# Constants of an S5 branch on GpSimd alone and half-swapped key and query rows in a one-core decoder step

## The chip, the cores and the metric

One core of a Trainium2 chip runs the whole program. The metric is device time in microseconds (us), the median of several runs; one further execution was profiled. All products are float32 in and out.

## The reference, cut to what matters

A hybrid decoder layer is computed for one prompt (16 meta tokens and 512 tokens) and, with the same weights, for 8 single-token samples: a normalised x times a wide input weight gives queries, keys, values, an S5 input u and gates; the two branches are merged through gates and two output weights, and a last weight leads back to x.

```python
h = jnp.einsum('btd,de->bte', rmsnorm(x, norm_gain), w_in)      # 2048 -> q, k, v, z_a, u, z_s, g_a, g_s
q = rope(rmsnorm(q, q_norm_gain), pos); k = rope(rmsnorm(k, k_norm_gain), pos)
...
x1 * cos - x2 * sin, x2 * cos + x1 * sin                        # rope: the two halves of a head cross
...
lam_bar = jnp.exp(lam * dt)                                     # the constants of the S5 branch
b_bar = ((lam_bar - 1.0) / lam)[..., None] * lax.complex(b_re, b_im)
a_cum, h = lax.associative_scan(ssm_combine, (a, bu), axis=1)
...
br_a = (o_attn * jax.nn.silu(z_a)) @ w_attn_out
br_s = (y_ssm * jax.nn.silu(z_s)) @ w_ssm_out
return x + (jax.nn.sigmoid(g_a) * br_a + jax.nn.sigmoid(g_s) * br_s) @ w_out
```

Attention is over a window of 128 positions, the 16 meta tokens and a sink.

## The kernel before, in words

Every float32 product is three matmuls of rounded parts: ScalarE casts a weight to a high part (whi), VectorE subtracts it to get the low part (wlo), and TensorE multiplies high by high, high by low and low by high. The weights come as 176 units of 512 KB through SP's queue into three buffers (`Stream`, L961 to L963) and each is used for 48 matmuls of 260 columns.

The stages on TensorE, one after the other: blocks of plain products (`mm`, L1116); from 114 to 394 us thirteen "quads" (`Quads`, `quad`, L1319), in which seven products do the work of eight: sums of weight tiles are made on VectorE (L1024) and sums of x, the "taus", ahead of time (`taus`, L1378 to L1398); then again plain blocks (q, k, v heads, u, gates), beside which the S5 scan and, from 754 us on, the attention run; the output weights; a last group of quads.

Work beside the products is written as generators in the lanes of a `Background` (L906). Every 24 matmuls `bg.step(budget)` runs the lanes on until the costs they yield use up a budget (`BUDGET2` to `BUDGET4` from the attention on); `yield None` ends a lane's turn in that step. So where a piece of background work stands in the order of each engine is set by the costs and budgets, and each engine and each queue goes through its list in order. The loads and splits of weights have a higher priority (`HIGH`) and go in front.

What the change and the prediction touch: `ssm_prep` (L143) makes the constants of the S5 branch during the quads, tensor_tensor and tensor_scalar on GpSimd and everything else (scalar_tensor_tensor, reciprocal) on VectorE, through the class `Mostly` (L30); in its middle TensorE transposes F (L225), and the result goes out through SP (L231). `again` (L1428) then stores the constants that are kept (983 KB) on SP's queue (L1430). `heads` (L1270) writes each block of q, k or v rows to DRAM (`rawD`, L1277); `Attn.load` (L619) reads a block back (`sb`), once more with the 32-row quarters exchanged in pairs (`sw`, four pieces, L628), and the norms (`rb`, L631); `rope` (L637) combines the three, `queries` (L709) makes QT (L718, L719), and `scores` (L723) multiplies (L735, L736). `sample_heads` (L556) does the same for the samples on GpSimd's queue. `attention` (L1516) orders all this.

```python
# in attention()
         at.load_q(0)
         yield None
         for kv in range(4):
             yield from at.queries(kv)
             yield from at.blocks(kv, kv == 3)
```

Of the kernel before, what the change touches and what calls it, by code (L numbers as in the profile page):

```python
# [8 lines left out]
F32 = mybir.dt.float32  # L9
# [3 lines left out]
ALU = mybir.AluOpType  # L13
# [13 lines left out]
    return a.to_broadcast(s)  # L27


class Mostly:  # L30


    def __init__(self, a, b):
        self.a, self.b = a, b

    def __getattr__(self, name):
        return getattr(self.a if name in ("tensor_tensor", "tensor_scalar", "tensor_copy", "memset") else self.b, name)


def acc_exp(v, pool, out, x, n):  # L40
# [73 lines left out]

def spots():

    r, o = {("early", "size"): 704, ("prod", "size"): 512, ("late", "size"): 256, ("pow", "size"): 192}, 0
    for nm, n in (("ex_c", 32), ("ex_k", 32), ("ex_r", 32), ("ex_q", 32), ("ex_i", 32), ("sc_n", 64), ("sc_k", 64), ("sc_r", 64),
                  ("sc_s", 64), ("sc_q", 64), ("f_g", 64), ("f_m", 32), ("f_t", 32), ("f_n", 32)):
        r[nm] = ("early", o)  # L120
        o += n
    r["nta"] = ("early", 0)
    for nm, o in (("c96_1", 0), ("c96_2", 192), ("ct1", 0), ("ct2", 256)):
        r[nm] = ("prod", o)
    for nm, o in (("fts", 0), ("Z", 0), ("zc", 64), ("zc2", 128), ("n32a", 192)):
# [16 lines left out]

def ssm_prep(nc, K, tmp, psum, dram, R, ident, a_prm, later):  # L143

    v = Mostly(nc.gpsimd, nc.vector)
    prm = K["prm"]
    nc.sync.dma_start(out=prm, in_=a_prm)
    are, aim, ldt = prm[:, 0], prm[:, 1], prm[:, 2]
    dt = tmp.tile([P, 32], F32, name="dt")
    acc_exp(v, tmp, dt, ldt, 32)  # L150
    yield 3.0
# [43 lines left out]
    m2 = tmp.tile([P, 32], F32, name="f_m")
    t = tmp.tile([P, 32], F32, name="f_t")
    v.tensor_tensor(out=m2, in0=are, in1=are, op=ALU.mult)
    v.tensor_tensor(out=t, in0=aim, in1=aim, op=ALU.mult)
    v.tensor_tensor(out=m2, in0=m2, in1=t, op=ALU.add)
    v.reciprocal(out=m2, in_=m2)  # L200
# [15 lines left out]
    nF = K["nF"]  # L216
    v.tensor_scalar(out=nF, in0=fv[:, :, 0], scalar1=-1.0, scalar2=None, op0=ALU.mult)
    yield 2.5
    for _ in range(6):
        yield None  # L220
    ft = psum.tile([P, 512], F32, name="tr")
    fts = tmp.tile([P, 2, P], F32, name="fts")
    with later():
        for h in range(2):
            nc.tensor.transpose(out=ft[:, 128 * h:128 * h + 128], in_=Fk[:, 4 * h:4 * h + 4].rearrange("p k a -> p (k a)"),  # L225
                                identity=ident)
    yield 0.0
    yield None
    nc.scalar.copy(out=fts.rearrange("p h s -> p (h s)"), in_=ft[:, 0:256])
    FD = dram.tile([8, 32, P], F32, name="FD")  # L230
    nc.sync.dma_start(out=FD.rearrange("(h k) a s -> (k a) h s", h=2), in_=fts)  # L231
    R["FD"] = FD
    yield 0.0
# [322 lines left out]
def sample_heads(nc, pool, dram, smc, idn, raw, rk, rq, ps, later):  # L556

    v = nc.vector
    x, sw, rb = (pool.tile([P, 12, 8], F32, name=n, bufs=1) for n in ("x12", "s12", "r12"))
    qs, kvs = (pool.tile([P, n, 8], F32, name=nm, bufs=1) for nm, n in (("qs", 8), ("kvs", 4)))  # L560
    for c in range(2):
        cols = slice(4 * c, 4 * c + 4)
        src = raw[:, :, c, 264:268].rearrange("n p j -> p n j")
        nc.gpsimd.dma_start(out=x[:, :, cols], in_=src)
        for q in range(4):
            b = 32 * (q ^ 1)
            nc.gpsimd.dma_start(out=sw[32 * q:32 * q + 32, :, cols], in_=src[b:b + 32])
# [36 lines left out]
class Attn:  # L604
# [14 lines left out]
    def load(self, i, W, row):  # L619

        nc, pool = self.nc, self.pool
        cs = slice(CH - W, CH)
        sb = pool.tile([P, 2, W], F32, name="sb")
        nc.sync.dma_start(out=sb, in_=self.raw[i][:, :, cs])
        sw = pool.tile([P, 2, W], F32, name="sw")
        for q in range(4):
            b = 32 * (q ^ 1)
            nc.sync.dma_start(out=sw[32 * q:32 * q + 32], in_=self.raw[i][b:b + 32, :, cs])  # L628
        rb = pool.tile([P, 2 * W], F32, name="rb")
        for e in range(2):  # L630
            nc.sync.dma_start(out=rb[64 * e:64 * e + 64], in_=row(e).unsqueeze(0).to_broadcast([64, 2 * W]))  # L631
        return sb, sw, rb
# [52 lines left out]
    def values(self, e):  # L685
        nc, pool = self.nc, self.pool
        sb = pool.tile([P, 2, CH], F32, name="sv")
        nc.sync.dma_start(out=sb, in_=self.raw[2 + e])
# [351 lines left out]
def trunk(tc, A, O):  # L1040
# [229 lines left out]
    def heads(i):  # L1270
# [156 lines left out]

    def again():  # L1428

        nc.sync.dma_start(out=kD, in_=flats[0][:, 0:NKEPT])  # L1430
        quarters()
        raw = [qs.more.tile([P, 8, P], F32, name="raw", bufs=3).rearrange("p k n -> p (k n)") for _ in range(3)]
        raw = [raw[n // 3][:, CH * (n % 3):CH * (n % 3) + CH] for n in range(8)]
        for n, r in enumerate(raw):
            nc.sync.dma_start(out=r, in_=A["x"][:, 2 * n, 1])
        yield 0.0
        yield None
        for n, r in enumerate(raw):
            list(xkeep(2 * n, r, 1))
            yield 0.5  # L1440
# [75 lines left out]
    def attention():  # L1516
# [341 lines left out]
```

## Time and profile before

| | us |
|---|---|
| median of 3 runs | 1291.26 (1290.59 to 1296.47) |
| profiled execution, own time | 1291.91 |
| its span | 1290.1 |
| TensorE busy | 1263.1 (98%), 10405 matmuls |
| VectorE busy | 966.4 (75%) |
| ScalarE busy | 622.6 (48%) |
| GpSimd busy | 240.0 (19%) |
| DMA | 215.94 MB, mean 167 GB/s |

The span is the profiled part of one execution; its own time is some 1.8 us longer, and stands 0.65 us over the median. Busy shares are averages over stages that differ, so where time is lost has to be read by stretches. The granted clock of TensorE was 0.991 of full over the span.

### The profile page before, as it was taken

How to read it: one execution, taken by the hardware profiler on the slowest of the kernel's cores; microseconds unless marked ns; L12 is line 12 of the kernel's file. 1: busy time of each engine (PE TensorE's matmuls, PEld its weight loads, DVE VectorE, ACT ScalarE, POOL GpSimd, SP SyncE). 2: the span in 40 equal slices, each digit the busy share in tenths (PEclk: the TensorE clock that was granted, in tenths of full speed). 3: DMA queues.
4: the chain of work that ended last, by engine and by line, in shares of the span. 5: the costliest groups of instructions: out<-in, count | busy, mean ns of one | idle time of the engine just before them, and what ended most of it. 6: DMA issues, size and time to landing. Idle time of an engine off the chain costs nothing.

```text
span 1290.1 us, 26491 instructions
## 1 busy us (share of the span) xinstructions
PE 1263.1 (98%) x10405; PEld 1236.8 (96%) x10405; DVE 966.4 (75%) x1536; ACT 622.6 (48%) x1330; POOL 240.0 (19%) x420
## 2 busy tenths in 40 slices
PE   9999899999999999999999997999999999999998
PEld 9999899999999999999999997999999999999998
DVE  8586598687786578877679648889976567887775
ACT  8554354345455864455522233486556623344442
POOL 0003899700001420122033221111110000000000
PEclk9999899999999999999999998999999999999999
DMA  8544243244346545545454479777874565545441
GB/s 287 201 153 163 91 134 134 103 157 157 114 129 226 175 128 174 160 140 157 132 144 119 136 214 279 225 237 220 234 251 149 166 192 182 181 153 156 143 145 51
DMA packets 104274, 215.94 MB, mean 167 GB/s; under 512 B 21740, under 2 KB 43172, under 8 KB 104116
## 3 DMA queue, kind: packets, MB, share of 16 engines
q1 hardware_dynamic: 95700, 196.83, 47.7%
q0 software_dynamic: 8448, 17.40, 5.6%
q8 instruction: 82, 1.34, 0.5%
q14 instruction: 44, 0.36, 0.1%
HBM read 180.99 MB, written 34.11 MB: 167 GB/s over the span
## 4 chain that ended last, share of the span: by engine, by line
PE 77%; POOL 11%; issue 6%; DMA 3%; ACT 1%; DVE 1%; SPq 1%; POOLq 0%; ACTq 0%; DVEq 0%
PE mm L1116 46%; PE pr L1319 22%; POOL work L69 2%; PE wg L784 2%; POOL work L71 2%; POOL work L70 1%; DMA raw<-in_w 1%; DMA xr<-in_x 1%; PE aux L1116 1%; POOL work L72 1%; POOL work L57 1%; PE aux L1319 1%; POOL work L56 1%; PE wg L515 1%; PE tr L515 1%
## 5 line engine op out<-in xcount | busy, mean ns | idle before, releaser
L1025 ACT CAST whi<-raw 128x1024 fp32r<-128x1024 f32 x147 | 151.9, 1048 | 158.9 <-DVE raw L1024 80.9
L1026 DVE TENSOR_TENSOR wlo<-raw,whi 128x1024 fp32r<-128x1024 f32 x147 | 182.9, 1266 | 56.6 <-ACT whi L1025 56.2
L962 ACT CAST whi<-raw 128x1024 fp32r<-128x1024 f32 (+3 forms) x136 | 130.7, 970 | 171.1 <-PE mm L1116 93.9
L1116 PE MATMUL mm<-xh,whi 128*128 128x260 f32 (+1 forms) x888 | 207.1, 287 | 1.7 <-ACT xr L1174 1.7
L1116 PE MATMUL mm<-xh,wlo 128*128 128x260 f32 (+1 forms) x888 | 205.5, 285 | 0.0
L1116 PE MATMUL mm<-xl,whi 128*128 128x260 f32 (+1 forms) x888 | 204.1, 284 | 0.0
L963 DVE TENSOR_TENSOR wlo<-raw,whi 128x1024 fp32r<-128x1024 f32 (+3 forms) x136 | 152.1, 1126 | 63.1 <-ACT whi L962 53.1
L1319 PE MATMUL pr<-cb,whi 128*128 128x260 f32 x848 | 153.1, 283 | 1.8 <-ACT whi L1025 1.8
L1116 PEld LDWEIGHTS mm<-xh,whi 128*128 128x128 f32 x888 | 147.6, 189 | 5.6 <-issue 2.5
L1319 PE MATMUL pr<-tau,whi 128*128 128x260 f32 x800 | 146.1, 284 | 3.5 <-ACT z L1353 2.3
L1116 PEld LDWEIGHTS mm<-xh,wlo 128*128 128x128 f32 x888 | 147.6, 189 | 1.1 <-issue 1.0
L1116 PEld LDWEIGHTS mm<-xl,whi 128*128 128x128 f32 x888 | 148.0, 189 | 0.0
L1319 PEld LDWEIGHTS pr<-cb,whi 128*128 128x128 f32 x848 | 130.9, 189 | 2.0 <-ACT whi L1025 2.0
L1319 PEld LDWEIGHTS pr<-tau,whi 128*128 128x128 f32 x800 | 123.7, 189 | 3.9 <-ACT z L1353 2.5
L1319 PE MATMUL pr<-cb,wlo 128*128 128x260 f32 x424 | 119.1, 283 | 0.0
L1319 PE MATMUL pr<-tau,wlo 128*128 128x260 f32 x400 | 113.1, 283 | 0.0
L1024 DVE TENSOR_TENSOR raw<-raw 128x1024 f32<-128x1024 f32 x84 | 104.0, 1238 | 8.3 <-DMA raw<-in_w 6.9
L1116 PE MATMUL mm<-Y,whi 128*128 128x260 f32 x576 | 105.9, 288 | 0.3 <-DVE Y L1575 0.3
L1319 PE MATMUL pr<-xh,whi 128*128 128x260 f32 x304 | 85.4, 287 | 3.6 <-ACT whi L1025 3.5
L1116 PEld LDWEIGHTS mm<-Y,whi 128*128 128x128 f32 x576 | 83.8, 188 | 3.4 <-issue 2.7
L1319 PE MATMUL pr<-xh,wlo 128*128 128x260 f32 x304 | 86.3, 285 | 0.6 <-DVE wlo L1026 0.6
L1319 PE MATMUL pr<-xl,whi 128*128 128x260 f32 x304 | 86.1, 285 | 0.0
(421 smaller groups left out, 2968.5 us busy)
## 6 DMA issues: line engine op xcount, KB each, us to landing
raw<-in_w SPq DMA_DIRECT2D x202, 512.0 KB, 4.3
gD<-z SPq DMA_DIRECT2D x38, 260.0 KB, 4.4
t<-gD SPq DMA_DIRECT2D x32, 260.0 KB, 2.8
cache<-in_vc POOLq DMA_DIRECT2D x16, 286.0 KB, 3.9
cache<-in_kc POOLq DMA_DIRECT2D x15, 288.0 KB, 5.9
xr<-in_x SPq DMA_DIRECT2D x16, 268.0 KB, 5.0
xg<-in_x SPq DMA_DIRECT2D x8, 536.0 KB, 4.7
sD<-z SPq DMA_DIRECT2D x16, 260.0 KB, 2.9
```

Of the source, the lines that this page charges most:

```text
L56: v.tensor_tensor(out=q, in0=q, in1=r, op=ALU.mult)
L69: v.tensor_tensor(out=t1, in0=a, in1=bc(br, 1, 2), op=ALU.mult)
L71: v.tensor_tensor(out=out[:, 0], in0=t1[:, 0], in1=t2[:, 1], op=ALU.subtract)
L515: nc.tensor.matmul(o[n], lhsT=D["CL"][:, 2 * e + n, i, 1:5], rhs=H[:, 2 * e + n, i, 0:140], start=False, stop=(i == 1))
L784: nc.tensor.matmul(pv[64 * e:64 * e + 64, 0:256], lhsT=V, rhs=pr[:, e::2], start=(i == 0), stop=(i == len(parts) - 1))
L962: nc.scalar.copy(out=hi, in_=raw)
L963: self.dve = nc.vector.tensor_tensor(out=lo, in0=raw, in1=hi.bitcast(F32), op=ALU.subtract).ins
L1024: nc.vector.tensor_tensor(out=o, in0=o, in1=i, op=ALU.add)
L1025: nc.scalar.copy(out=hi, in_=t)
L1026: nc.vector.tensor_tensor(out=lo, in0=t, in1=hi.bitcast(F32), op=ALU.subtract)
L1116: m = nc.tensor.matmul(ps[:, c, 0:W], lhsT=wt[:, k], rhs=xo(kt, c), start=f, stop=l)
L1319: m = nc.tensor.matmul(bank, lhsT=wt[:, p], rhs=x(p, e), start=first and f and p == 0, stop=l and p == 7, skip_group_check=not first and l ...
```

## The change

- The class `Mostly` becomes `OnPool`: a scalar_tensor_tensor of the constants is now a tensor_scalar and a tensor_tensor, both on GpSimd. The reciprocal of |lambda|^2 stays on VectorE, its input is made first, and seven idle turns stand behind it.
- F's transposes, copy and store go from the middle of the constants to their end, behind eight idle turns.
- The kept constants are stored through GpSimd's queue.
- `rawD` holds each block twice. `heads` stores k and q also with quarters exchanged, in four pieces of 32 partitions; `load` reads both copies with 128 partitions each into one tile `sbw`. `sample_heads` reads the second copy as well.
- The loads of x for the taus stand under an order behind the last background matmul.
- Two idle turns (`NDELAY`) stand between the first queries and the first scores; three budgets are larger.

```diff
-class Mostly:
+class OnPool:
...
+    def scalar_tensor_tensor(self, out, in0, scalar, in1, op0, op1):
+        n = int(np.prod(out.shape[1:]))
+        t = self.tmp.tile([P] + list(out.shape[1:]), F32, name=f"st{n}")
+        self.e.tensor_scalar(out=t, in0=in0, scalar1=scalar, scalar2=None, op0=op0)
+        self.e.tensor_tensor(out=out, in0=t, in1=in1, op=op1)
...
-    v = Mostly(nc.gpsimd, nc.vector)
+    v = OnPool(nc, tmp)
...
+    v.tensor_tensor(out=m2, in0=are, in1=are, op=ALU.mult)
+    v.tensor_tensor(out=t, in0=aim, in1=aim, op=ALU.mult)
+    v.tensor_tensor(out=m2, in0=m2, in1=t, op=ALU.add)
+    yield 0.0
+    for _ in range(7):
+        yield None
+    v_ = nc.vector
+    v_.reciprocal(out=m2, in_=m2)
...
-    for _ in range(6):
-        yield None
-    ft = psum.tile([P, 512], F32, name="tr")
...
+    for _ in range(8):
+        yield None
+    ft = psum.tile([P, 512], F32, name="tr")
...
-        sb = pool.tile([P, 2, W], F32, name="sb")
-        nc.sync.dma_start(out=sb, in_=self.raw[i][:, :, cs])
-        sw = pool.tile([P, 2, W], F32, name="sw")
-        for q in range(4):
-            b = 32 * (q ^ 1)
-            nc.sync.dma_start(out=sw[32 * q:32 * q + 32], in_=self.raw[i][b:b + 32, :, cs])
+        t = pool.tile([P, 2, 2, W], F32, name="sbw")
+        for k in range(2):
+            nc.sync.dma_start(out=t[:, k], in_=self.raw[i][k][:, :, cs])
+        sb, sw = t[:, 0], t[:, 1]
...
-BUDGET2, BUDGET3, BUDGET4 = 5.2, 2.8, 4.2
+BUDGET2, BUDGET3, BUDGET4 = 5.6, 3.0, 4.6
+NDELAY = 2
...
-        nc.sync.dma_start(out=rawD[i][:, :, CH - W:], in_=sb)
+        nc.sync.dma_start(out=rawD[i][0][:, :, CH - W:], in_=sb)
...
+        for q in range(4):
+            b = 32 * (q ^ 1)
+            nc.sync.dma_start(out=rawD[i][1][b:b + 32, :, CH - W:], in_=sb[32 * q:32 * q + 32])
...
-                nc.sync.dma_start(out=xgs[p], in_=A["x"][:, 2 * p:2 * p + 2])
+                with tc.issue_after(bg.last):
+                    nc.sync.dma_start(out=xgs[p], in_=A["x"][:, 2 * p:2 * p + 2])
...
-        nc.sync.dma_start(out=kD, in_=flats[0][:, 0:NKEPT])
+        nc.gpsimd.dma_start(out=kD, in_=flats[0][:, 0:NKEPT])
...
             yield from at.queries(kv)
+            if kv == 0:
+                for _ in range(NDELAY):
+                    yield None
             yield from at.blocks(kv, kv == 3)
```

How the order moves at three places. On VectorE, among the first quads, before (L51, L52, L173 and L175 are steps of the constants, L200 is the reciprocal, raw<-raw a sum of weights, wlo a split):

```order
L1026 TENSOR_TENSOR wlo<-raw,whi 128x1024
L1024 TENSOR_TENSOR raw<-raw 128x1024
L200 RECIPROCAL work<-work 128x32
L51 SCALAR_TENSOR_TENSOR work<-work 128x32
L1026 TENSOR_TENSOR wlo<-raw,whi 128x1024
L52 SCALAR_TENSOR_TENSOR work<-work 128x32
...
L1026 TENSOR_TENSOR wlo<-raw,whi 128x1024 x4
L51 SCALAR_TENSOR_TENSOR work<-work 128x32
L1024 TENSOR_TENSOR raw<-raw 128x1024
L52 SCALAR_TENSOR_TENSOR work<-work 128x32
L173 SCALAR_TENSOR_TENSOR work<-work 128x64
L1024 TENSOR_TENSOR raw<-raw 128x1024
```

And with the change, from the same split of the first quad on (L165 is the reciprocal):

```order
L1035 TENSOR_TENSOR wlo<-raw,whi 128x1024
L165 RECIPROCAL work<-work 128x32
L1033 TENSOR_TENSOR raw<-raw 128x1024
L1035 TENSOR_TENSOR wlo<-raw,whi 128x1024 x2
L1033 TENSOR_TENSOR raw<-raw 128x1024
L1035 TENSOR_TENSOR wlo<-raw,whi 128x1024 x4
L1033 TENSOR_TENSOR raw<-raw 128x1024 x2
```

The single steps of the constants are gone from between the sums and splits, and the reciprocal stands one sum of weights earlier.

On SP's queue, around the store of the kept constants, before (L1006 is a weight load of the quads, L1153 a store of a block's gate, L1430 the store of the constants):

```order
L231 DMA FD<-work 128x2x128
L1153 DMA gD<-t 128x520
L1006 DMA raw<-in_w 128x1024 x4
L1153 DMA gD<-z 128x520
L1430 DMA kept<-work 128x1920
L1153 DMA gD<-z 128x520
L1006 DMA raw<-in_w 128x1024 x4
```

The same place on SP with the change:

```order
L1162 DMA gD<-t 128x520 x2
L1015 DMA raw<-in_w 128x1024 x4
L1162 DMA gD<-z 128x520 x2
L1015 DMA raw<-in_w 128x1024 x4
```

The two transfers of constants are gone from between the weight loads.

On TensorE, around the first scores, before (L735 and L736 are the scores, mm a block of gates, whi_9848 and wlo_9849 one weight unit):

```order
L1116 MATMUL mm_9994<-xh_81,wlo_9849 128x260
L1116 MATMUL mm_9994<-xhq_4522,wlo_9849 128x260
L1116 MATMUL mm_9994<-xh_81,whi_9848 128x260 x2
L1116 MATMUL mm_9994<-xl_82,whi_9848 128x260 x2
L735 MATMUL aux_9879<-KH0_9379,QT0_9767 128x272
L736 MATMUL aux_9879<-KL0_9383,QT0_9767 128x272
L1116 MATMUL mm_9994<-xh_81,wlo_9849 128x260 x2
```

With the change (L743 and L744 are the scores):

```order
L1125 MATMUL mm_9820<-xh_81,whi_9745 128x260 x2
L1125 MATMUL mm_9820<-xl_82,whi_9745 128x260 x2
L1125 MATMUL mm_9820<-xh_81,wlo_9746 128x260
L743 MATMUL aux_9923<-KH0_9399,QT0_9741 128x272
L744 MATMUL aux_9923<-KL0_9403,QT0_9741 128x272
L1125 MATMUL mm_9820<-xh_81,wlo_9746 128x260
L1125 MATMUL mm_9993<-xh_81,whi_9822 128x260
```

The first score stood ten matmuls into a weight unit; now it stands one matmul short of the end of an earlier unit. Counted from the start, 3418 matmuls of plain blocks stood ahead of it, and 3359 now.

## Rows read from the trace of the kernel before

**Rows 1.** Busy time, share of the span and instructions of each engine, first part of the page

```profile
PE 1263.1 (98%) x10405; PEld 1236.8 (96%) x10405; DVE 966.4 (75%) x1536; ACT 622.6 (48%) x1330; POOL 240.0 (19%) x420
```

**Rows 2.** 50 us stretches: length, busy (count) of PE, PEld, DVE, ACT, POOL; clock, DMA, GB/s

```profile
100.00:150.00 50.00, 46.74 (x366) 46.22 (x365) 33.10 (x39) 18.46 (x25) 29.84 (x60) 0.93 0.35 120
150.00:200.00 50.00, 48.83 (x407) 48.62 (x406) 40.45 (x40) 22.11 (x31) 48.35 (x74) 1.00 0.42 136
200.00:250.00 50.00, 50.00 (x418) 50.00 (x418) 42.01 (x38) 21.42 (x30) 48.31 (x57) 1.00 0.23 77
250.00:300.00 50.00, 45.73 (x361) 44.93 (x360) 37.09 (x37) 22.78 (x32) 0.00 (x0) 0.93 0.52 179
750.00:800.00 50.00, 43.08 (x350) 42.87 (x349) 32.27 (x56) 15.71 (x30) 11.94 (x25) 0.93 0.94 260
850.00:900.00 50.00, 50.00 (x407) 46.13 (x406) 45.83 (x89) 34.68 (x96) 6.27 (x12) 1.00 0.71 214
```

**Rows 3.** VectorE's timeline: start, us, line, operation, [idle before it <-releaser]

```profile
134.20 0.20 DVE L51 SCALAR_TENSOR_TENSOR work<-work 128x32 f32<-128x32 f32 x1 [5.62 <-POOL work L50]
```

**Rows 4.** Waits of SP's queue: line waited for, us in total, times, longest

```profile
SPq L1430 <- POOL work L287: 23.7, 1, 23.7
```

**Rows 5.** SP's timeline at the store of the kept constants

```profile
248.74 0.33 SPq L1430 DMA_DIRECT2D kept<-work  x1
```

**Rows 6.** VectorE's timeline behind that store

```profile
255.39 1.22 DVE L1024 TENSOR_TENSOR raw<-raw 128x1024 f32<-128x1024 f32 x1 [6.95 <-DMA raw<-in_w]
```

**Rows 7.** Waits of all engines, at the first scores

```profile
PE aux L735 <- DVE QT L719: 6.9, 1, 6.9
```

**Rows 8.** Stretches of 5 us, columns as in rows 2

```profile
160.00:165.00 5.00, 3.83 (x32) 3.62 (x31) 4.96 (x7) 1.45 (x2) 4.83 (x8) 1.00 0.02 3
785.00:790.00 5.00, 4.83 (x41) 4.62 (x39) 2.83 (x4) 1.05 (x1) 0.58 (x1) 1.00 1.25 264
790.00:795.00 5.00, 0.00 (x0) 0.00 (x0) 4.13 (x8) 1.34 (x3) 0.00 (x0) 0.82 0.92 279
795.00:800.00 5.00, 3.25 (x15) 3.25 (x16) 4.90 (x7) 1.98 (x3) 0.55 (x1) 0.50 0.96 272
800.00:805.00 5.00, 5.00 (x43) 5.00 (x43) 4.91 (x9) 2.29 (x3) 0.74 (x2) 1.00 1.08 314
```

**Rows 9.** GpSimd's timeline, without and with work on VectorE beside it

```profile
131.66 0.25 POOL L59 TENSOR_TENSOR work<-work 128x32 f32<-128x32 f32 x1
...
138.19 1.28 POOL L57 TENSOR_SCALAR work<-work 128x32 f32<-128x32 f32 x1
```

**Rows 10.** SP's timeline at the attention's loads

```profile
754.27 0.90 SPq L688 DMA_DIRECT2D sv<-rawD  x2
...
776.35 0.57 SPq L624 DMA_DIRECT2D sb<-rawD  x1
...
777.83 2.84 SPq L628 DMA_DIRECT2D sw<-rawD  x4
```

**Rows 11.** The stretch of those loads, columns as in rows 2

```profile
754.00:786.00 32.00, 32.00 (x271) 32.00 (x271) 21.15 (x40) 10.32 (x24) 10.73 (x23) 1.00 0.94 267
```

**Rows 12.** VectorE's timeline ahead of the first scores

```profile
785.26 0.76 DVE L642 SCALAR_TENSOR_TENSOR sb<-sb,k_attc 128x520 f32<-128x520 f32 x1 [0.57 <-DMA sb<-rawD]
785.93 1.22 DVE L963 TENSOR_TENSOR wlo<-raw,whi 128x1024 fp32r<-128x1024 f32 x1
...
790.87 0.76 DVE L643 SCALAR_TENSOR_TENSOR sw<-sw,k_attc 128x520 f32<-128x520 f32 x1 [2.79 <-DMA sw<-rawD]
791.55 0.69 DVE L645 TENSOR_TENSOR sb<-sb,sw 128x520 f32<-128x520 f32 x1
...
792.83 0.75 DVE L651 TENSOR_TENSOR sw<-sb,rb 128x256 f32<-128x256 f32 x2
...
796.01 1.40 DVE L719 TENSOR_TENSOR QT<-sw,QT 64x512 fp32r<-64x512 f32 x2
```

**Rows 13.** VectorE's timeline, a weight split beside GpSimd

```profile
245.67 2.16 DVE L1026 TENSOR_TENSOR wlo<-raw,whi 128x1024 fp32r<-128x1024 f32 x1 [0.50 <-ACT whi L1025]
```

More of the change, by code (lines that the diff above doesn't have):

```diff
@@ L27, in bc, with __init__ @@
     return a.to_broadcast(s)
-class Mostly:
-    def __init__(self, a, b):
-        self.a, self.b = a, b
+class OnPool:
+    def __init__(self, nc, tmp):
+        self.e, self.tmp = nc.gpsimd, tmp
     def __getattr__(self, name):
-        return getattr(self.a if name in ("tensor_tensor", "tensor_scalar", "tensor_copy", "memset") else self.b, name)
+        return getattr(self.e, name)
+    def scalar_tensor_tensor(self, out, in0, scalar, in1, op0, op1):
[3 more added lines that the diff above has]
+        self.e.tensor_tensor(out=out, in0=t, in1=in1, op=op1)
 def acc_exp(v, pool, out, x, n):
@@ L115, in spots @@
 def spots():
-    r, o = {("early", "size"): 704, ("prod", "size"): 512, ("late", "size"): 256, ("pow", "size"): 192}, 0
+    r, o = {("early", "size"): 704, ("prod", "size"): 512, ("late", "size"): 192, ("pow", "size"): 192}, 0
     for nm, n in (("ex_c", 32), ("ex_k", 32), ("ex_r", 32), ("ex_q", 32), ("ex_i", 32), ("sc_n", 64), ("sc_k", 64), ("sc_r", 64),
-                  ("sc_s", 64), ("sc_q", 64), ("f_g", 64), ("f_m", 32), ("f_t", 32), ("f_n", 32)):
+                  ("sc_s", 64), ("sc_q", 64), ("f_g", 64), ("f_n", 32), ("st32", 32), ("st64", 64), ("m2", 32)):
         r[nm] = ("early", o)
@@ L122, in spots @@
     r["nta"] = ("early", 0)
-    for nm, o in (("c96_1", 0), ("c96_2", 192), ("ct1", 0), ("ct2", 256)):
+    for nm, o in (("c96_1", 0), ("c96_2", 192), ("ct1", 0), ("ct2", 256), ("fts", 0)):
         r[nm] = ("prod", o)
-    for nm, o in (("fts", 0), ("Z", 0), ("zc", 64), ("zc2", 128), ("n32a", 192)):
+    for nm, o in (("Z", 0), ("zc", 64), ("zc2", 128)):
         r[nm] = ("late", o)
@@ L148, in ssm_prep @@
     are, aim, ldt = prm[:, 0], prm[:, 1], prm[:, 2]
+    m2 = tmp.tile([P, 32], F32, name="m2")
+    t = tmp.tile([P, 32], F32, name="th")
+    v.tensor_tensor(out=m2, in0=are, in1=are, op=ALU.mult)
[6 more added lines that the diff above has]
+    v_.reciprocal(out=m2, in_=m2)
     dt = tmp.tile([P, 32], F32, name="dt")
@@ L194, in ssm_prep @@
     g = tmp.tile([P, 2, 32], F32, name="f_g")
[L195 to L200, printed above, removed]
     v.tensor_scalar(out=g[:, 0], in0=lam[:, 0], scalar1=1.0, scalar2=None, op0=ALU.subtract)
@@ L218, in ssm_prep @@
     yield 2.5
-    for _ in range(6):
-        yield None
-    ft = psum.tile([P, 512], F32, name="tr")
[L222 to L233, printed above, removed]
     r4 = K["r4"]
@@ L288, in ssm_prep @@
     yield 1.0
+    for _ in range(8):
+        yield None
+    ft = psum.tile([P, 512], F32, name="tr")
+    fts = tmp.tile([P, 2, P], F32, name="fts")
+    with later():
+        for h in range(2):
+            nc.tensor.transpose(out=ft[:, 128 * h:128 * h + 128], in_=Fk[:, 4 * h:4 * h + 4].rearrange("p k a -> p (k a)"),
+                                identity=ident)
+    yield 0.0
+    yield None
+    nc.scalar.copy(out=fts.rearrange("p h s -> p (h s)"), in_=ft[:, 0:256])
+    FD = dram.tile([8, 32, P], F32, name="FD")
+    nc.sync.dma_start(out=FD.rearrange("(h k) a s -> (k a) h s", h=2), in_=fts)
+    R["FD"] = FD
+    yield 0.0
 def ssm_states(nc, cst, pool, R, a_h0):
@@ L562, in sample_heads @@
         cols = slice(4 * c, 4 * c + 4)
-        src = raw[:, :, c, 264:268].rearrange("n p j -> p n j")
+        src, swap = (raw[:, k, :, c, 264:268].rearrange("n p j -> p n j") for k in range(2))
         nc.gpsimd.dma_start(out=x[:, :, cols], in_=src)
-        for q in range(4):
-            b = 32 * (q ^ 1)
-            nc.gpsimd.dma_start(out=sw[32 * q:32 * q + 32, :, cols], in_=src[b:b + 32])
+        for bl in (slice(0, 2), slice(4, 12)):
+            nc.gpsimd.dma_start(out=sw[:, bl, cols], in_=swap[:, bl])
         for e in range(2):
@@ L622, in load @@
         cs = slice(CH - W, CH)
-        sb = pool.tile([P, 2, W], F32, name="sb")
-        nc.sync.dma_start(out=sb, in_=self.raw[i][:, :, cs])
-        sw = pool.tile([P, 2, W], F32, name="sw")
-        for q in range(4):
-            b = 32 * (q ^ 1)
-            nc.sync.dma_start(out=sw[32 * q:32 * q + 32], in_=self.raw[i][b:b + 32, :, cs])
+        t = pool.tile([P, 2, 2, W], F32, name="sbw")
+        for k in range(2):
+            nc.sync.dma_start(out=t[:, k], in_=self.raw[i][k][:, :, cs])
+        sb, sw = t[:, 0], t[:, 1]
         rb = pool.tile([P, 2 * W], F32, name="rb")
@@ L687, in values @@
         sb = pool.tile([P, 2, CH], F32, name="sv")
-        nc.sync.dma_start(out=sb, in_=self.raw[2 + e])
+        nc.sync.dma_start(out=sb, in_=self.raw[2 + e][0])
         yield None
@@ L1262, in ssm @@
         load_u()
-    rawD = dram.tile([12, P, 2, CH], F32, name="rawD")
+    rawD = dram.tile([12, 2, P, 2, CH], F32, name="rawD")
     skD, rkD = (dram.tile([4, 2 * CH], F32, name=n) for n in ("skD", "rkD"))
@@ L1552, in attention @@
             yield from at.queries(kv)
+            if kv == 0:
+                for _ in range(NDELAY):
+                    yield None
             yield from at.blocks(kv, kv == 3)
```

## Prediction, made before the changed kernel was run

> **What bounds the kernel now.** First the busy line of the page [rows 1]: TensorE is busy 98% of the span, so almost nothing can be won but TensorE's own holes, and an edit that leaves those alone is worth nothing. Where the holes are is read from 50 us windows [rows 2]. Undisturbed, TensorE issues 418 matmuls in 50 us, 0.1196 us each (200 to 250 us). Three windows are short and a fourth a little: 366 in 100 to 150 (52 missing x 0.1196 = 6.2 us), 407 in 150 to 200 (1.3 us), 361 in 250 to 300 (6.8 us), 350 in 750 to 800 (8.1 us). Together that is 22.4 us. The 407 of 850 to 900 are no hole: TensorE is busy for all 50 us there, with the attention's own matmuls among them.
>
> Then what ends each hole. **Hole 1:** VectorE runs single steps of the constants between the weight splits, and waits for GpSimd in order, 5.62 us before the step at 134.20 [rows 3]. The sums of weights behind it come late. **Hole 2:** SP's queue waits 23.7 us in all at the store of the kept constants, for the last multiplication of GpSimd [rows 4]; it gets away at 248.74 [rows 5], a gD store and four weight loads stand right behind it in the queue, and VectorE waits 6.95 us for the first of them [rows 6]. **Hole 3:** TensorE waits 6.9 us at the first scores for QT [rows 7]. What an idle time costs beyond itself is in the 5 us windows [rows 8]: TensorE falls idle 0.17 us before 790, does nothing to 795, where the granted clock averages 0.82, has 3.25 us of work in the next window, which is at 0.50 whole, and the one after is at 1.00. So it went to its lower level (1.2 GHz) for some (0.18/0.5) x 5 + 5 = 6.8 us, from about 793.2, 3.4 us after it fell idle (789.83). The 1.17 us of idling at 160 to 165 left the clock at 1.00.
>
> **The change, part by part.** The sum is made against the profiled execution, 1291.9 us (span 1290.1); the median of the runs is 1291.26, 0.65 less. A measurement of this kernel can tell some 0.5%, 6.5 us, from no change.
>
> *Constants on GpSimd alone.* Eight scalar_tensor_tensor leave VectorE; the order of VectorE shows weight sums and splits behind one another where L51, L52, L173 and L175 stood. Only the reciprocal stays, moved to the front of the quads: it waits for GpSimd's first three operations, a sum of weights earlier than before. I bound that from nothing to 2.6 us (GpSimd's first operations against VectorE's arrival, about ten steps of 0.25 us [rows 9]) and take nothing, since two weight sums and a split already lie ahead of it. So holes 6.2 and 1.3 go: **-7.5 us**. GpSimd gets 16 operations for them, 0.25 us each alone and 1.28 us beside VectorE [rows 9]: 4 to 20.5 us more. It is busy 29.84 + 48.35 + 48.31 = 126.5 us from 100 to 250 [rows 2], so it is done at most 147 us after the quads began. The transposes of F now come after 1807 of the quads' 2184 matmuls, 1807 x 0.1196 = 216 us after they began: some 70 us of cover. If that were gone, TensorE would stand at the transposes, which are in its order. Their copy and SP transfer move with them, past the weight loads of all quads but the last; the first reader of FD comes behind the quads.
>
> *The store on GpSimd's queue.* Its wait for the last multiplication is now on the engine that does that multiplication, and SP's next gD store and four weight loads no longer stand behind it. Nothing stands behind it on GpSimd, which does nothing from 250 to 300 us [rows 2]. Cost nothing, gain hole 2: **-6.8 us**. The Trainium skill, "DMA: Bandwidth & Descriptors", section "Issuing engines are not separate DMA queues", says that starting transfers from several engines only saves the time to start them. By that rule the move would be worth the 0.33 us of one issue, and the sum would stay some 6.5 us higher; the wait row says otherwise, since it was no issue time that was lost but a place in an ordered queue.
>
> *Rows with halves swapped.* Ten head blocks store four more pieces of 32 partitions each, 40 SP issues. At the 0.57 to 0.71 us of one such transfer [rows 10] that is 23 to 28 us of SP, spread over 350 us behind the quads, and 2.7 MB, 10 us at the 267 GB/s of [rows 11]. Three weight buffers cover a piece of 4 x 0.7 = 2.8 us; without them each block could hold a weight load for that. I take nothing. The loads of the attention fall from 1 + 4 + 2 to 2 + 2 issues, with the same bytes. The sample heads' transfers on GpSimd halve; there is nothing waiting.
>
> *Sums of x.* On SP the xg loads stand exactly where they stood; an order tied to the last background matmul reaches only TensorE's own queue. Nothing.
>
> *First scores.* Two idle turns are added, but the three background budgets grow by 7 to 10%, and the order shows the net: 3359 matmuls of the x blocks ahead of the first score, before 3418. The score stands 59 x 0.1196 = 7.1 us **earlier**. TensorE would come to it at 789.83 - 7.1 = 782.8 in the clock of the old profile. The data: the attention's loads began at 754.27 [rows 10]; the scan ends about 22 matmuls earlier in the order, so 751.7. Ahead of the first query head lie two v, two k with swapped halves and norms (1.6 MB and 0.5), two key stores (0.5), four weight tiles (2.1), three other tiles (1.3), four cache tiles (1.2), and the head itself (0.8): about 8.0 MB, 30 us at 267 GB/s [rows 11]. Before, sb of that head was issued at 776.35, sw of the next head at 777.83 [rows 10]; VectorE stood 2.79 us for the latter at 790.87, with the first head's sum behind it [rows 12]. Now both halves are one tile and this crossing is gone: behind the landing stand two gains, a sum, the norms, a split and one QT, 0.76 + 0.76 + 0.69 + 0.75 + 1.22 + 0.7 = 4.9 us [rows 12]. Ready at 751.7 + 30 + 4.9 = 786.6, 3.8 us after TensorE. That is over the 3.4 us after which the clock fell, so the half clock runs from 786.2 to 793.0, 6.4 us of it under work, which costs half: 3.8 + 3.2 = 7.0 us against 8.1 now. **-1.1 us.** The wait's bounds are 0 and the old 6.9 plus 7.1 - 2.6 = 11.4 us (nothing of the loading gets faster).
>
> Sum: 1291.9 - 7.5 - 6.8 - 1.1 = 1276.5, and 0.65 off for the median: **1276 us**.
>
> **The rivals.**
> A. *The wait at the first scores ends too.* If the shorter list of issues lets the head arrive 1 to 4 us sooner than by bandwidth, the wait is 0 to 3 us and the clock stays: 1291.26 - 22.4 = 1268.9 to 1271.9, say 1270. For it: SP issued four pieces for 2.84 us [rows 10] where now are two. Against: 0.94 of the transfer engines' time was taken [rows 11], and the bytes are the same.
> B. *It grows.* Scores 7.1 us earlier, data only 2.6 us earlier: 11.4 us idle, the half clock wholly inside it, 3.3 us worse than now: 1291.26 - 14.3 + 3.3 = 1280. For it: the first query's single tile must wait for a key tile's store to land and its copies, where sw's buffer was free sooner.
> C. *VectorE becomes the bound (slower than before).* The budgets pack its background 7.7% denser (5.6 for 5.2), and it is at 45.83 of 50 us from 850 to 900 [rows 2]; 45.83 x 1.077 = 49.4. From 50 on, weight splits are late, and each such stall costs what hole 3 does, 8.1 us. Three of them, one per window to 950, give 1276 + 24 = 1300. Against: only the background part of those 45.83 us grows, not the splits.
> D. *GpSimd holds up VectorE's splits.* A split took 2.16 us beside GpSimd [rows 13], 1.22 alone [rows 12]; 16 more operations could hold VectorE for 16 x 0.94 = 15 us. It is idle 16.9 + 9.5 + 8.0 = 34 us from 100 to 250 [rows 2], so that fits, unless it falls in one place and makes one stall like hole 2, 6.8 us: 1283. The Trainium skill, "SBUF — State Buffer", section "Who interferes with whom", has the rule: an operation of VectorE with two inputs in SBUF and one of GpSimd that reads SBUF shut each other out. By it this change moves work the wrong way; the trace agrees that both get longer [rows 9, 13], but TensorE issued its full 418 from 200 to 250 with GpSimd busy for 48.31 us.
> E. *The change does not do what it says.* Of the sums of x that holds already (nothing moves), and the first scores move the other way. It bears on A to C and gives no time of its own.
>
> **How the numbers follow.** Forecast, holes 1 and 2 gone and 3 nearly unchanged, 1276 (1274 to 1278): 0.50. A, 1270: 0.21. B, 1280: 0.15. D, 1283: 0.07. C, 1300: 0.04. One of holes 1 and 2 left in part, 1280 to 1287: 0.03. The range goes from A's end to a little beyond D, 1268 to 1284, and leaves C and the tails out. Up to 1284.8 is faster by over 0.5%: 0.90. Within 0.5%, from D's and the last case's tails and a single stall of C: 0.06. Slower: 0.04, C in full.
>
> **What would show it.** Right: 50 us windows with 417 or more matmuls from 100 to 300; no wait of VectorE for GpSimd beyond the reciprocal's; no wait of SP for GpSimd; GpSimd's constants done between 241 and 269 us; TensorE's wait for QT near 4 us, with a half clock of some 7 us behind it. A shows by a wait below 3.4 us and a clock at 1.00 there, B by one of 9 us or more. C shows as waits of TensorE for wlo between 800 and 1000, D as splits over 2 us and matmuls missing before 270. Wrong would be any new idle time over 3 us in the head blocks (the 40 stores) or at the transposes.

## The result, and the profile after

The changed kernel takes 1273.54 us in the median of 4 runs (1272.26 to 1275.23), against 1291.69 us (1290.59 to 1296.47) for the kernel before, 4 runs too: a ratio of 0.9853, 95% interval 0.9826 to 0.9881. The profiled execution took 1273.75 us, its span is 1271.6 us. The page's busy line [rows 1] now reads:

```profile
PE 1256.8 (99%) x10405; PEld 1231.8 (97%) x10405; DVE 962.5 (76%) x1528; ACT 622.6 (49%) x1330; POOL 263.4 (21%) x433
```

The 50 us windows [rows 2] show where the time came from:

```profile
100.00:150.00 50.00, 50.00 (x419) 50.00 (x419) 36.88 (x37) 21.01 (x29) 32.21 (x51) 1.00 0.46 149
150.00:200.00 50.00, 50.00 (x419) 50.00 (x418) 41.08 (x43) 23.61 (x33) 48.13 (x75) 1.00 0.37 123
200.00:250.00 50.00, 50.00 (x418) 50.00 (x417) 41.77 (x38) 23.24 (x33) 49.92 (x67) 1.00 0.42 143
250.00:300.00 50.00, 50.00 (x418) 50.00 (x417) 42.54 (x43) 23.10 (x33) 16.91 (x16) 1.00 0.42 142
750.00:800.00 50.00, 47.42 (x384) 47.21 (x383) 42.69 (x71) 19.47 (x40) 9.14 (x17) 0.97 0.91 266
```

366 and 407 matmuls became 419 and 419, which is 65 x 0.1196 = 7.8 us; 361 became 418, 6.8 us; 350 became 384, 4.1 us. That is 18.7 us against the 18.2 by which the two profiled executions differ. In the head blocks, with the 40 added stores, TensorE idles for 0.03 us in all (400 to 750 us), against none before.

VectorE waits for GpSimd only at the reciprocal [rows 3], and the store of the constants leaves GpSimd's queue as soon as they are made [rows 4, 5]. VectorE's timeline, then GpSimd's:

```profile
117.58 0.35 DVE L165 RECIPROCAL work<-work 128x32 f32<-128x32 f32 x1 [1.36 <-POOL work L160]
```

```profile
265.06 1.19 POOL L283 TENSOR_TENSOR work<-work 128x64 f32<-128x64 f32 x1
266.55 0.83 POOL L1443 DMA_DIRECT2D kept<-work  x1 [0.31 <-POOL work L283]
```

GpSimd ends 18 us later than before (248.74). Nothing on SP waits for it any more.

At the first scores the wait [rows 7] and the 5 us stretches around it [rows 8] are:

```profile
PE aux L743 <- DVE QT L727: 2.6, 1, 2.6
```

```profile
765.00:770.00 5.00, 2.62 (x23) 2.41 (x21) 4.17 (x7) 1.62 (x3) 0.00 (x0) 0.99 1.08 318
770.00:775.00 5.00, 4.80 (x28) 4.80 (x29) 4.90 (x9) 1.06 (x2) 0.58 (x1) 0.67 0.90 278
775.00:780.00 5.00, 5.00 (x45) 5.00 (x44) 5.00 (x9) 2.54 (x4) 0.55 (x1) 1.00 0.83 248
```

TensorE falls idle at 767.62, the score comes at 770.2, and the clock is at its lower level for some 0.01/0.5 x 5 + 0.33/0.5 x 5 = 3.4 us. SP's and VectorE's timelines ahead of it [rows 10, 12]:

```profile
735.02 1.34 SPq L696 DMA_DIRECT2D sv<-rawD  x2
...
754.74 1.35 SPq L635 DMA_DIRECT2D sbw<-rawD  x2
```

```profile
765.73 0.76 DVE L651 SCALAR_TENSOR_TENSOR sbw<-sbw,k_attc 128x520 f32<-128x520 f32 x1 [2.92 <-DMA sbw<-rawD]
766.53 0.70 DVE L653 TENSOR_TENSOR sbw<-sbw 128x520 f32<-128x520 f32 x1
...
769.46 0.68 DVE L727 TENSOR_TENSOR QT<-sbw,QT 64x512 fp32r<-64x512 f32 x1
```

From the first load of the attention to the end of the first QT it took 770.14 - 735.02 = 35.1 us; before it was 754.27 to 796.7, 42.4 us. This stretch is called the chain of loads below.

### The profile page after: what moved, and what is told of

The parts are those of the page before. It is cut to its first block, busy times and chain, and to the rows that moved or that the text cites. A ratio compares the mean times of both kernels' runs of the same rounds, so it can differ in the third digit from the quotient of the medians.

```text
span 1271.6 us, 26500 instructions
## 1 busy us (share of the span) xinstructions
PE 1256.8 (99%) x10405; PEld 1231.8 (97%) x10405; DVE 962.5 (76%) x1528; ACT 622.6 (49%) x1330; POOL 263.4 (21%) x433
## 4 chain that ended last, share of the span: by engine, by line
PE 87%; issue 5%; DMA 3%; ACT 2%; POOL 1%; DVE 1%; SPq 0%; POOLq 0%; ACTq 0%; DVEq 0%
PE mm L1125 46%; PE pr L1331 32%; PE wg L792 1%; PE aux L1331 1%; PE aux L1125 1%; DMA xr<-in_x 1%; PE tr L526 1%; PE wg L526 1%; DMA raw<-in_w 1%; DMA cache<-in_kc 1%; PE aux L743 0%; PE tr L774 0%; PE tr L469 0%; PE wg L469 0%; PE aux L744 0%
## 5 line engine op out<-in xcount | busy, mean ns | idle before, releaser
L1035 DVE TENSOR_TENSOR wlo<-raw,whi 128x1024 fp32r<-128x1024 f32 x147 | 181.3, 1254 | 62.1 <-ACT whi L1034 61.5
L1033 DVE TENSOR_TENSOR raw<-raw 128x1024 f32<-128x1024 f32 x84 | 105.2, 1252 | 1.4
L1125 PE MATMUL mm<-xhq,whi 128*128 128x260 f32 (+1 forms) x296 | 84.6, 286 | 0.0
```

The source lines that it names most:

```text
L1033: nc.vector.tensor_tensor(out=o, in0=o, in1=i, op=ALU.add)
L1035: nc.vector.tensor_tensor(out=lo, in0=t, in1=hi.bitcast(F32), op=ALU.subtract)
L1125: m = nc.tensor.matmul(ps[:, c, 0:W], lhsT=wt[:, k], rhs=xo(kt, c), start=f, stop=l)
```

## The experiments

Three sets of four kernels, each set timed beside the kernel before on one chip; ratios are to that set's kernel before (1289.6, 1290.6 and 1291.1 us). Differences in us are worked out from the ratios; those of the medians are up to 1 us away. Of each kernel one execution was profiled, so a wait below is that of one execution. First, single parts put into the kernel before.

### The store alone

```diff
-        nc.sync.dma_start(out=kD, in_=flats[0][:, 0:NKEPT])
+        nc.gpsimd.dma_start(out=kD, in_=flats[0][:, 0:NKEPT])
```

> The kernel before with one edit: the kept constants are stored through GpSimd's queue. Theory (the hole at 250 to 300 us came from a place in SP's ordered queue): that window fills to 417 or 418 matmuls, the holes at 100 to 200 and at the first scores stay, time 1291.7 - 6.8 = 1284.9 us. Rival (only the 0.33 us of the issue is saved, the weight loads were late for another reason): 361 matmuls there as before, 1291.4 us.

Measured: 1283.71 us, ratio 0.9948 (0.9926 to 0.9969), 6.7 us less. The window that had 361 matmuls is full:

```profile
250.00:300.00 50.00, 50.00 (x419) 50.00 (x418) 39.60 (x39) 24.91 (x36) 1.32 (x3) 1.00 0.48 163
```

The theory holds: the interval is 4.0 to 9.5 us. That its middle meets the 6.8 us of the forecast to a tenth is luck. What the queue had lost was a place in line, not the 0.33 us of an issue.

### The constants on GpSimd alone, with the store left on SP

```diff
-    v = Mostly(nc.gpsimd, nc.vector)
+    v = OnPool(nc, tmp)
...
+    for _ in range(8):
+        yield None
     ft = psum.tile([P, 512], F32, name="tr")
...
         nc.sync.dma_start(out=kD, in_=flats[0][:, 0:NKEPT])
```

> The kernel before with the constants on GpSimd alone and F's transposes at their end, but the store still on SP's queue. Theory (the parts depend on each other): the hole at 100 to 200 us goes (-7.5), but in this order the store stands five weight loads earlier on SP, about where the changed kernel's SP is at 190 us, while GpSimd ends later; SP waits until GpSimd is done, 35 us if its operations run at 0.3 us once VectorE starves, up to 75 us if not. Of the old wait of 23.7 us TensorE lost 6.8, so about 15 us are covered: it loses 20 to 60 us in one hole, time 1297 to 1337 us, likeliest 1300. Rival (the parts simply add): the wait costs 6.8 us as before, 1284 us.

Measured: 1303.77 us, ratio 1.0104 (1.0086 to 1.0122), so slower by 13.4 us and within the theory's range. SP's wait, SP's timeline around it, TensorE's wait, VectorE's, and four stretches:

```profile
SPq L1442 <- POOL work L283: 48.6, 1, 48.6
```

```profile
182.44 1.60 SPq L1018 DMA_DIRECT2D raw<-in_w  x2
232.76 0.33 SPq L1442 DMA_DIRECT2D kept<-work  x1
```

```profile
PE pr L1331 <- DVE z L1366: 27.3, 1, 27.3
```

```profile
238.88 2.48 DVE L1036 TENSOR_TENSOR raw<-raw 128x1024 f32<-128x1024 f32 x2 [30.01 <-DMA raw<-in_w]
```

```profile
210.00:215.00 5.00, 4.46 (x38) 4.25 (x36) 0.00 (x0) 0.38 (x1) 5.00 (x16) 1.00 0.00 0
215.00:220.00 5.00, 0.00 (x0) 0.00 (x0) 0.00 (x0) 0.00 (x0) 5.00 (x18) 0.95 0.00 2
...
235.00:240.00 5.00, 0.00 (x0) 0.00 (x0) 1.12 (x1) 0.00 (x0) 0.00 (x0) 0.50 0.99 325
240.00:245.00 5.00, 3.25 (x15) 3.25 (x16) 4.88 (x7) 1.65 (x2) 0.00 (x0) 0.50 0.69 278
```

SP stood from 184 to 232.8 with weight loads behind the store; the hole cost (418 - 171) x 0.1196 = 29.5 us in the window from 200 to 250, while the holes at 100 to 200 (420 and 418 matmuls) and at 250 to 300 (418) are gone. The parts do not add: this one is 13.4 us slower alone, the store alone 6.7 us faster, and both together 15 us faster (below). With GpSimd doing more, the store has to leave the place that it had on SP's queue.

### The rows stored twice, alone

```diff
-        for q in range(4):
-            b = 32 * (q ^ 1)
-            nc.sync.dma_start(out=sw[32 * q:32 * q + 32], in_=self.raw[i][b:b + 32, :, cs])
+        for k in range(2):
+            nc.sync.dma_start(out=t[:, k], in_=self.raw[i][k][:, :, cs])
...
+            nc.sync.dma_start(out=rawD[i][1][b:b + 32, :, CH - W:], in_=sb[32 * q:32 * q + 32])
```

> The kernel before with only the rows stored twice and read back in two loads. The first scores stand 4 matmuls later than before. Theory (the shorter list of loads lets the first query head arrive several us sooner; the changed kernel's wait of 2.6 us was only so long because its scores stand 59 matmuls earlier): no or hardly any wait at the first scores, 750 to 800 us window at 410 or more matmuls, 1291.7 - 8.1 = 1283.6 us. Rival (the bytes are the same, and the arrival is by bandwidth): wait 4 to 7 us, 1287 to 1292 us.

Measured: 1292.89 us, ratio 1.0021 (1.0011 to 1.0032). The wait is 5.9 us, so the theory fell and the rival holds for the wait; the kernel is 0.2% slower, clear of the noise, for which 1.0 us of a new wait of TensorE at a transpose between 650 and 700 us is a part and the rest is open. SP's and VectorE's timelines:

```profile
755.68 0.90 SPq L685 DMA_DIRECT2D sv<-rawD  x2
...
779.63 3.60 SPq L624 DMA_DIRECT2D sbw<-rawD  x4
```

```profile
791.08 0.76 DVE L640 SCALAR_TENSOR_TENSOR sbw<-sbw,k_attc 128x520 f32<-128x520 f32 x1 [1.25 <-DMA sbw<-rawD]
791.75 0.75 DVE L639 SCALAR_TENSOR_TENSOR sbw<-sbw,k_attc 128x520 f32<-128x520 f32 x1
...
797.51 1.40 DVE L716 TENSOR_TENSOR QT<-sbw,QT 64x512 fp32r<-64x512 f32 x2
```

The first QT took 42.5 us from the first load, as before. The loads of both heads go out together 24 us after the start (19.7 us in the changed kernel, for one head), and the second head's steps stand before the first QT: 7.1 us from the last landing to its end, against 4.4.

### The budgets and idle turns alone

```diff
-BUDGET2, BUDGET3, BUDGET4 = 5.2, 2.8, 4.2
+BUDGET2, BUDGET3, BUDGET4 = 5.6, 3.0, 4.6
```

> The kernel before with only the three budgets and the two idle turns. The first scores stand 33 matmuls (3.9 us) earlier. Theory (budgets move the scores towards data that do not come sooner): wait 7 to 11 us, 1292 to 1296 us. Rival (larger budgets also bring the loads forward by as much): 1291.7 us, wait 6 to 7 us.

Measured: 1295.32 us, ratio 1.0037 (1.0024 to 1.0051). The time is as the theory had it, the cause is not: the wait at the first scores shrank to 3.6 us (the loads did move forward), but others came, 2.3 us at the gates' products among them:

```profile
PE aux L735 <- DVE QT L719: 3.6, 1, 3.6
PE mm L1116 <- DVE Y L1578: 2.3, 2, 2.0
```

This profile also lost 16 matmuls more than the kernel before in the stall of the store (345 from 250 to 300 us, and 361 there), 1.9 us. The edit acts only from the attention on, so this is not its doing.

### What the other parts add to constants and store

The second set starts from the changed kernel. All four have the constants on GpSimd and the store on its queue.

```diff
-BUDGET2, BUDGET3, BUDGET4 = 5.6, 3.0, 4.6
+BUDGET2, BUDGET3, BUDGET4 = 5.2, 2.8, 4.2
...
-        t = pool.tile([P, 2, 2, W], F32, name="sbw")
+        sb = pool.tile([P, 2, W], F32, name="sb")
...
+        sw = pool.tile([P, 2, W], F32, name="sw")
```

Both edits make the first kernel, which has no idle turns and no order on the sums of x either; the budgets alone (and no idle turns) make the second, the storage alone the third.

> The changed kernel with only the constants on GpSimd alone and their store on its queue: rows stored once, old budgets, no idle turns, no order on the sums of x. Theory (these two parts alone carry the gain of the holes at 100 to 300 us, the rest is worth the 3.5 us that the attention lost less): 418 matmuls in each window from 100 to 300, wait at the first scores 5 to 7 us, 14.3 us under the kernel before, ratio 0.989. Rival (the wait at the first scores depends on how loads happen to fall, and the rest of the change is worth nothing): wait 2 to 3 us as in the changed kernel, ratio 0.9855.

> The changed kernel with the old budgets and no idle turns. Theory (twice stored rows gain only together with the budgets: alone, the loads of the first two query heads go out together and both heads' steps stand before the first QT): wait at the first scores 5 to 7 us, first QT 42 us after the first load of the attention, ratio 0.989 to 0.990. Rival (the score 63 matmuls later meets data that come as early as in the changed kernel): no wait, ratio 0.982.

> The changed kernel with rows stored once and read back in five loads. Theory (budgets alone move loads and scores together): first QT 40 us after the first load of the attention, wait 3 to 5 us, further waits of 2 to 3 us in the attention as in the run with the budgets alone, ratio 0.990. Rival (the storage is worth nothing, the budgets bring the gain): wait 2.6 us, ratio 0.9855.

The fourth has the idle turns taken out:

```diff
-NDELAY = 2
+NDELAY = 0
```

> The changed kernel with NDELAY at 0. The first score stands 4 matmuls later instead of 59 earlier minus those, so at the same place. Theory (the idle turns do not move the first scores, the budgets do): wait 2 to 3 us, ratio 0.985 to 0.9865. Rival (the idle turns keep other work away from VectorE before the first QT): wait 5 us or more, ratio 0.988 or more.

Measured:

| constants and store, and | us | ratio (95%) | wait at first scores |
|---|---|---|---|
| nothing | 1275.32 | 0.9879 (0.9865 to 0.9892) | 0.4, and 2.1 at a transpose before |
| rows twice | 1278.72 | 0.9907 (0.9892 to 0.9923) | 5.8 |
| budgets, idle turns | 1277.96 | 0.9901 (0.9884 to 0.9919) | 4.2 |
| rows twice, budgets | 1271.09 | 0.9850 (0.9837 to 0.9862) | none |
| all (the changed kernel, its own set) | 1273.54 | 0.9853 (0.9826 to 0.9881) | 2.6 |

Constants and store alone bring 0.0121 x 1290.6 = 15.6 us of the gain, though without the wait of 5 to 7 us that I expected. There TensorE had lost time at a transpose at 751 us (2.1 us, and 3.4 us at the lower clock behind it), so it came to the first scores 39.8 us after the first load and met data that took 40.1 us; before it came after 35.6 us. The wait at the first scores is a race between the two, and a late TensorE hides late data.

Rows stored twice or larger budgets alone add nothing, and by their middle values take 3 us. Their waits are as expected; with the budgets alone the chain of loads took 41.8 us, where I expected 40. Both together are under constants and store by some 3.7 us, with intervals that just do not meet (for the changed kernel itself, which has the idle turns too, they overlap). Part of that is the clock, which differs between executions of one kernel: three of the four runs with constants and store alone had a mean clock of 0.996 or 0.997, and the one at 0.999 took 1272.81 us, 0.4 us over the slowest of the four runs with both. The idle turns are worth nothing in time that could be seen, as expected; that the wait of 2 to 3 us would stay without them was not borne out.

### Where the loads fall

The third set tries to tell why, and whether what is left can be won. The first kernel is that with rows twice and the old budgets, with one turn before the keys' work; the second is the changed kernel with two, and the third the changed kernel with four idle turns instead of two. The edit of the first:

```diff
         keys = at.keys(O["k"])
+        for _ in range(1):
+            yield None
```

> The kernel of pool_store_swap with one idle turn between the issue of the keys' loads and their work. The first score stands 35 matmuls (4.2 us) earlier than there, and on SP the first query head's loads stand alone, with the second head's two places later. Theory (where the loads and steps of the first two heads fall among the weight loads and background turns decides how long the first QT takes, not the storage by itself): first QT 38 us or less after the first load of the attention, against 42.6 there, wait 0 to 4 us, ratio 0.985 to 0.988. Rival (the data come by bandwidth alone, so an earlier score waits longer): wait 8 to 10 us, ratio 0.992 or more.

Measured: 1275.51 us, ratio 0.9886 (0.9867 to 0.9905). SP's first load of the attention and that of the first query head, and VectorE's first QT:

```profile
739.53 0.90 SPq L696 DMA_DIRECT2D sv<-rawD  x2
...
764.06 1.26 SPq L635 DMA_DIRECT2D sbw<-rawD  x2
```

```profile
774.68 0.69 DVE L727 TENSOR_TENSOR QT<-sbw,QT 64x512 fp32r<-64x512 f32 x1
```

The same three in the kernel without the turn, where the loads of two query heads go out together:

```profile
738.80 0.90 SPq L696 DMA_DIRECT2D sv<-rawD  x2
...
762.75 3.42 SPq L635 DMA_DIRECT2D sbw<-rawD  x4
```

```profile
780.72 1.40 DVE L727 TENSOR_TENSOR QT<-sbw,QT 64x512 fp32r<-64x512 f32 x2
```

35.8 us to the end of the first QT, where the kernel without the turn took 42.6, and a wait of 2.5 us though the score stands 4.2 us earlier. So with the same storage, bytes and budgets, one idle turn takes 6.8 us off the chain of loads: the theory is borne out in the trace. The first head's loads went out no sooner (24.5 us after the first load, 24.0 without the turn); what got shorter is the time from there to QT, 11.3 instead of 18.7 us, with one head's transfers and steps ahead of it and not two. The ratio is 0.002 better than without the turn, with intervals that overlap, and by its middle value a little above the theory's range.

The 6.8 us is more than this chain moves by itself. In the four kernels with rows stored once and the old budgets it took 38.8 to 42.4 us; with rows stored twice alone 42.5 and 42.6; with both, or with the idle turn, 32.8 to 35.8 over six kernels.

> The changed kernel with two idle turns between the issue of the keys' loads and their work; the first score stands 25 matmuls (3.0 us) later than there. Theory (the wait of 2.6 us and its half clock are what is left of the hole): no wait over 1 us at the first scores, 410 or more matmuls from 750 to 800, ratio 0.982 to 0.983. Rival (what is won there comes back as waits within the attention, since its chain of softmax and turns is pressed together): ratio 0.985 or more, with other waits of TensorE adding up to 3 us or more between 750 and 950.

> The changed kernel with NDELAY at 4: the first score stands 25 matmuls (3.0 us) later, the keys' work where it was. Theory as for the kernel before this: no wait over 1 us at the first scores, ratio 0.982 to 0.983. Rival: the attention's chain gives it back, ratio 0.985 or more.

Measured: 1273.37 us, ratio 0.9876 (0.9855 to 0.9897), and 1270.96 us, ratio 0.9855 (0.9834 to 0.9876). Neither waits at the very first score any more. Both wait at the first scores of the second query head, the first for 2.1 us at 784.10 and the second for 0.8 us at 779.26, and the clock stays at 1.00 in both places. The first kernel's QT of both heads on VectorE, and its wait:

```profile
769.60 0.68 DVE L727 TENSOR_TENSOR QT<-sbw,QT 64x512 fp32r<-64x512 f32 x1
...
783.27 1.40 DVE L727 TENSOR_TENSOR QT<-sbw,QT 64x512 fp32r<-64x512 f32 x2
```

```profile
PE aux L743 <- DVE QT L727: 2.1, 1, 2.1
```

So the hole at the first score can be closed, but the rival holds for the time: with 388 and 397 matmuls from 750 to 800 us, where 410 were expected, both ratios are 0.985 or more. In the first, other waits of TensorE add up to 2.3 us up to 950 us, where the rival had 3 or more. The second's profiled span is the shortest of all, 1268.5 us, but the runs don't show the expected 3 us. It lost part of it near 1115 us, to the clock. Its stretches, and then those of the changed kernel around the same idle time:

```profile
1110.00:1115.00 5.00, 3.24 (x28) 3.03 (x27) 4.57 (x5) 3.79 (x6) 0.00 (x0) 1.00 0.22 65
1115.00:1120.00 5.00, 5.00 (x29) 5.00 (x30) 3.47 (x4) 1.17 (x3) 0.00 (x0) 0.66 0.42 148
```

```profile
1115.00:1120.00 5.00, 3.25 (x27) 3.04 (x26) 4.92 (x5) 3.79 (x7) 0.00 (x0) 1.00 0.30 96
1120.00:1125.00 5.00, 5.00 (x44) 5.00 (x44) 4.70 (x6) 1.08 (x2) 0.00 (x0) 1.00 0.37 119
```

No version that beats the changed kernel is shown.

### The transposes at their old place

```diff
+    for _ in range(6):
+        yield None
     ft = psum.tile([P, 512], F32, name="tr")
...
     r4 = K["r4"]
```

> The changed kernel with F's transposes, copy and store at the old place in the middle of the constants (955 quad matmuls ahead of them instead of 1903). Theory (the move is worth nothing: in the changed kernel's trace GpSimd finished F at 187 us, and the transposes would come near 217 us): no wait at the transposes, no wait of SP over 5 us at the store of F, ratio 0.984 to 0.987. Rival (GpSimd, now longer, is behind there, and SP's ordered queue waits for the copy with weight loads behind it): a hole of 3 us or more between 200 and 300, ratio 0.988 or more.

Measured: 1274.53 us, ratio 0.9883 (0.9858 to 0.9909). The windows from 100 to 300 are full (420, 418, 418 and 418 matmuls) and SP waits 1.6 us for the copy: no hole came, so the theory holds in the trace. By the ratio, which reaches from the changed kernel's to 0.991, it isn't settled. This profile shows something else too: its attention is that of the changed kernel, but the chain of loads took 32.8 us and the wait at the first scores was 0.2 us, against 35.1 and 2.6. So these differ by some 2 us without any edit in the attention.

## Why the prediction was right, point by point

- **Holes 1 and 2** were sized rightly: -7.5 and -6.8 forecast, 7.8 and 6.8 found. GpSimd ended at 266.6 (241 to 269 forecast), but "at most 147 us after the quads began" did not hold: it was 152.7. The 16 added operations took 10.5 us (two lines of 8, 5.9 and 4.6), between the bounds of 4 and 20.5; GpSimd's busy time from 100 to 300 us grew by 20.7 us (126.5 to 147.2), so its other operations grew by some 10 us, which the forecast left out. The reciprocal waited 1.36 us, and TensorE noticed nothing. F's transposes ran at 331.06, 64 us behind GpSimd's end, where I had put 70 us of cover. The 40 stores, taken at nothing, cost nothing (0.03 us of idling from 400 to 750 us).
- **The two parts as separate terms** were a mistake that the sum hides. "Cost nothing, gain hole 2: -6.8" is what the store is worth in the kernel before (6.7 alone). Beside the constants on GpSimd it is worth far more: without it that part ends 13.4 us slower than before. I had looked at where the store stood in the new order of GpSimd, and not at what the larger work would have done to SP's old queue; only the experiment's expectation did that.
- **The rule on issuing engines** of the Trainium skill ("DMA: Bandwidth & Descriptors", section "Issuing engines are not separate DMA queues"), by which the move would save one issue, gave the wrong size: 6.7 us for a transfer that issues in 0.33. The rule counts the time to start a transfer; lost here was the time in which a transfer that could not start yet held up those behind it (SP's wait of 23.7 us [rows 4]).
- **The first scores**: the forecast of the data was good (34.9 us from the first load to QT, 35.1 measured), TensorE came 1.5 us later after that load than forecast (32.6 against 31.1), so the wait was 2.6 instead of 3.8 us. What failed in size is the next step, "the half clock runs from 786.2 to 793.0": it lasted 3.4 us and not 6.8, and it began some 2.3 us after TensorE fell idle and not 3.4. The term was -1.1 and came out as -4.1. Those 3.0 us, and 0.3 at hole 1, are more than the 2.5 us between 1276 and 1273.5. There is luck in the term: the same attention had a wait of 0.2 us in the kernel with the transposes at their old place.
- **The cause given for that term fell**: "this crossing is gone" is true with rows stored twice alone as well, and there QT took 42.5 us as before. Only together with a shift of the background turns did the chain get shorter, by the budgets or by one idle turn. That my 30 us by bandwidth met the result is luck and not the cause: the same bytes took 33 to 43 us.
- **The rivals.** A: the wait was below its 3.4 us, but the clock fell, so the gain was half of A's. B is out. C: no slower kernel and no wait for wlo, but a trace of it is there: budgets alone made the kernel before 0.4% slower, with waits after the first scores; the changed kernel waits 1.1 us for VectorE's scores at 814 and idles for 1.6 us from 850 to 950, where TensorE was busy throughout before. D is out: single splits still took over 2 us (the longest 2.15, before 2.38), but over both groups of quads splits took 1254 ns in the mean, 1266 before, and sums of weights 1252, before 1238, with GpSimd busy for 23 us more, and TensorE missed nothing. So here what the Trainium skill's rule of the shared port ("SBUF — State Buffer", section "Who interferes with whom") describes cost GpSimd time, not TensorE: in the kernel that stood still, without VectorE's work beside them, GpSimd's constants were through at 232.8, not 266.6.
- **E**: the two idle turns did nothing that the time shows, and the edit of the sums of x left the window before the quads as it was (1.00 clock, 419 matmuls from 50 to 100, 418 before); no run tests that edit by itself.

## What to carry to other kernels

A transfer that waits for a slow producer belongs on that producer's queue, not on the one that feeds the critical engine; what the move is worth depends on how late the producer is, so such edits are to be sized together and not one by one. Where an engine waits for the end of a chain of loads and small steps, the end can come 7 us sooner or later with the same bytes, by where the chain falls among the other queue entries: look at what was issued in between and whose steps stand first, before storage is rearranged. After single stalls, count what the clock took behind them, and give it a range.

## What was not expected of the hardware

The lower clock did not last equally long. After 6.9 us of idling it was there for 6.8 us [rows 8], after 2.58 us for 3.4 us (770 to 775 above), and it was down even after an idle time of 1.76 us (29 matmuls instead of 44 from 1115 to 1120 in the kernel with four idle turns, 0.34/0.5 x 5 = 3.4 us), while an idle time that differs by 0.01 us left the changed kernel's clock at 1.00. That last wait, 1.8 us for ScalarE in the last group of quads, stands in all fourteen profiles of this case; behind it the clock fell in seven of them and stayed at 1.00 in the other seven. Nor does the longer wait decide: behind 2.06 us (the wait until 784.10 above) the clock stayed, behind the 2.13 us at the transpose with constants and store alone it fell. Over the waits at the first scores, 0.2 to 3.6 us left nothing or 3.4 us of lower clock, and 4.2 to 6.9 us left 6.8. What tells these apart is open; at 1.8 us of idling it makes some 1.7 us (half of 3.4) of difference between two executions.
